# A two-layer diffusion trunk: TensorE's order in both mixers, changed

## The chip, the cores and the metric

The kernel runs on one core of one Trainium2 chip. TensorE (PE) multiplies matrices, VectorE (DVE), ScalarE (ACT) and GpSimd (POOL) do the rest, and SyncE (SP) issues the transfers. The metric is the device time of one launch in microseconds (us). Three runs of the kernel before took 1543.56, 1544.5 and 1545.21 us; the median is 1544.5.

## The reference

The reference is one step of a trunk with two layers, for 128 context tokens and 256 latent tokens, 1024 wide. Each layer is half a SwiGLU, two mixers side by side whose outputs share one projection, and half a SwiGLU again; each sublayer is modulated by a condition.

```
layer 0: h += swiglu(...)/2;  h += [GQA with qk-RMSNorm and axial rotary || bidirectional mLSTM] @ W_mix;   h += swiglu(...)/2
layer 1: h += swiglu(...)/2;  h += [2-D neighbourhood attention with bias || sliding-window GQA with sink] @ W_mix;  h += swiglu(...)/2
attention:  s = q @ k.T * scale (+ bias, + sink column);  p = softmax(s);  o = p @ v
```

Every attention has 8 heads of 64. Latent queries read latent keys (a window of them in layer 1) and 128 cached context keys; context queries read the context alone. The mLSTM replaces the softmax by a decay: exp of differences of cumulated gate logs, forward and backward, times q @ k.T.

## The kernel before

**Tiles and weights.** Tokens lie in three tiles of 128: T=0 is the context, T=1 and T=2 are latent. Weights are streamed: a transfer on SP brings a block into one of three `raw` buffers, ACT makes its high part `whi` (line 121) and DVE or POOL the low part `wlo` (line 122), and each product is three matmuls of 384 columns (lines 378 to 380): high times high, low times high, high times low. One such triple is a *step*; 8 triples, 24 matmuls, make one projection of 128 features (`feat_major`, tile `fm`).

**What sets the order.** A scheduler orders the instructions of each engine by a simulated timeline. Inside a region `in_order` (line 61) the instructions of the engines named are chained in the order in which the code issues them; here that is TensorE. The first mixer has no such region, the loop of the second has one.

**First mixer (layer 0, 300 to 505 us).** The table `ORDER0` (line 30) lists its parts: `k` projects the query tile of two mLSTM heads (`qk_b`, line 934; the copy to `qb` at line 935 and the stacked halves `ksb`, `qdb`), `p` is mLSTM part 1, with `decay` for each head (line 959: two tiles D from `sel` and a mask, then six exponentials on ACT, line 973), `g` the output gate, `f` part 2, `a` the attention of a pair of heads, `m` the output projection. The same table sets the order of the weight blocks. Ahead of it the queries and keys of the attention are normalised, rotated by `rope` (line 610, three operations on DVE for each call) and *turned*: transposed by TensorE into tile `tr` and split into high and low halves `qs`, `ks` on ACT and DVE (lines 645 to 690).

**Second mixer (layer 1, 1069 to 1245 us).** There are 24 attention items: four pairs of heads of sliding-window attention, then four of neighbourhood attention, each with T=1, T=2 and T=0 in this order. An item has three parts (`attn`, line 695): *scores* (tile S, and behind it on DVE and ACT the bias or the sink, the maximum `nm`, the exponential, the sum, and the scaling of E at line 633), *turn* (E transposed into `pt`, line 719, and copied to PT by ACT), and *output* (PT times values into a part of the first `pt` bank, line 732, then split by ACT and DVE into `ych`, `ycl` or `ydh`, `ydl`, lines 636 to 638). Two banks hold `pt`. Between the parts, `fill(n)` sets n steps of other projections (first `fm`, later `mo`). `FILL` gives their numbers for T=1, T=2 and T=0.

Of the kernel before, what the change touches and what calls it, by code (L numbers as in the profile page):

```python
# [6 lines left out]
F32 = mybir.dt.float32  # L7
# [19 lines left out]

ORDER0 = "k0 p0 k1 p1 a0 g0 f0 a1 k2 p2 g1 f1 a2 k3 p3 g2 f2 a3 g3 f3 m0"  # L30

FILL = ((1, 2), (1, 2), (0, 1))
BIG = 1e30


# [101 lines left out]
def body(ctx, tc, d):  # L137
# [469 lines left out]
    def heads(ap, n=64):  # L607
        return ap.rearrange("p (h e) -> p h e", e=n)

    def rope(pool, src, ct, st, nh, nw=4):  # L610

        u, v = work(pool, 512, bufs=nw), work(pool, 512, bufs=nw)
        n = nh * 64
        nc.vector.tensor_tensor(heads(u[:, :n]), heads(src), ct[:, None, :].to_broadcast([P, nh, 64]), op=ALU.mult)
        s4 = src.rearrange("p (h a e) -> p h a e", a=2, e=32)[:, :, ::-1, :]
        v4 = v[:, :n].rearrange("p (h a e) -> p h a e", a=2, e=32)
        t4 = st.rearrange("p (a e) -> p a e", a=2)[:, None, :, :].to_broadcast([P, nh, 2, 32])
        nc.vector.tensor_tensor(v4, s4, t4, op=ALU.mult)
        nc.vector.tensor_tensor(u[:, :n], u[:, :n], v[:, :n], op=ALU.add)
        return u[:, :n]  # L620

    def soft(pool, S, n, nk):

# [139 lines left out]
    def run(steps):  # L763
        finish()
        for _ in steps:
            pass
# [9 lines left out]
    def mixer0():  # L776
        with ExitStack() as es:
# [12 lines left out]
            vctx = m0v[:, 309:437]  # L790
            cbd = m0v[:, 437:1477].rearrange("p (a b) -> p a b", a=4)


            o = token_major(h, 288)
            kv = mp.tile([P, 3, 256], F32, name="kv")
# [97 lines left out]
            for T in TS:  # L893
                for w, (src, nh, h0) in enumerate(((qr[:, T], 8, 0), (kv[:, T, 0:128], 2, 8))):
                    rs = ss[:, T, h0:h0 + nh, None].to_broadcast([P, nh, 64])
                    nc.vector.tensor_tensor(heads(src), heads(src), rs, op=ALU.mult)
                    if T == 0:
                        nc.vector.tensor_tensor(heads(src), heads(src), qkg[:, w, None, :].to_broadcast([P, nh, 64]),
                                                op=ALU.mult)
                        if w == 1:  # L900
                            nc.sync.dma_start(d["k0"], src)
                        r = src
                    else:
                        r = rope(mp, src, cg[:, T - 1, w], sg[:, T - 1, w], nh)
                    (sk.queries if w == 0 else sk.keys)(r, T)

            YA = [(mp.tile([P, NT], F32R, name=f"yah{i}"), mp.tile([P, NT], F32R, name=f"yal{i}")) for i in range(4)]
            YB = []
# [10 lines left out]

            va = mp.tile([P, 3, 8, 65], F32, name="va")  # L920
            nc.vector.memset(va[:, :, :, 64:65], 1.0)
            o = token_major(h, 512)
            for T in range(3):
                nc.scalar.activation(va[:, T, :, 0:64], heads(o[T]), AF.Copy)
            qb = mp.tile([P, 4, NT], F32, tag="qb", name="qb")
            og = mp.tile([P, 4, NT], F32, tag="qo", name="og")

# [5 lines left out]

            def qk_b(i):
                nc.scalar.activation(qb[:, i], feat_major(h), AF.Copy)
                ks = mp.tile([P, 2, NT], F32R, tag="ksb", name="ksb", bufs=1)
                qd = mp.tile([P, 2, NT], F32R, tag="qdb", name="qdb", bufs=1)
                for j in range(2):
                    stack_q(ks[:, j], kb[:, i], j, 1.0)
                    stack_k(qd[:, j], qlb[0][:, j], qb[:, i], j, lambda d, s: nc.gpsimd.tensor_copy(d, s))  # L940
                qkb[i] = ks, qd, qlb[0]

            wst = mp.tile([P, 8, 2], F32, name="wst")
            hst = {}
            sel = mp.tile([P, 64], F32R, name="sel")
            nc.vector.tensor_tensor(sel, ident[:, 0:64], ident[:, 64:128], op=ALU.add)
            mmb = mp.tile([P, 2, 3 * P], BF, name="mmb")
            nc.vector.tensor_copy(mmb.rearrange("p d (b t) -> p d b t", b=3), mmask[:, :, None].to_broadcast([P, 2, 3, P]))
            headg2 = mp.tile([P, 4], F32, name="headg2")
            nc.vector.tensor_scalar(headg2, headg, 0.5, None, op0=ALU.mult)  # L950


            MASKED = ((0, 0, 1), (0, 2, 4), (1, 0, 3))
# [5 lines left out]
            def decay(hd):  # L959
# [14 lines left out]
                nc.vector.tensor_copy(wst[:, hd], E.rearrange("p a n -> p (a n)")[:, 127:513:385])  # L974
                return E

            def part1(i):
                H = work(mp, 780, "H", 780, 2).rearrange("p (t x e) -> p t x e", t=3, e=65)
                for j in range(2):
                    hd = 2 * i + j  # L980
                    b = slice(64 * j, 64 * j + 64)
                    Hj = H[:, 1:3, 2 * j:2 * j + 2]
                    E = decay(hd)
                    pin = bank("ml", "pin")
                    for T in (1, 2):
                        nc.tensor.matmul(pin[:, (T - 1) * 130:T * 130], qb[b, i, T * P:(T + 1) * P],
                                         cbd[b, i, 130 * j:130 * j + 130], start=True, stop=True)
                    ks, qd, ql = [t[:, j] for t in qkb[i]]
                    products(pin[:, 260:388], ks[:, 0:P], qd[:, 0:P], ql[:, 0:P], P)
                    nc.vector.tensor_tensor(Hj, pin[:, 0:260].rearrange("p (t x e) -> p t x e", t=2, e=65),  # L990
                                            wi[:, :, hd, :, None].to_broadcast([P, 2, 2, 65]), op=ALU.mult)
                    nc.vector.tensor_tensor(E[:, :, 0:P], E[:, :, 0:P], pin[:, None, 260:388].to_broadcast([P, 2, P]),
                                            op=ALU.mult)
                    S = bank("ml", "Sm")
                    for o, T in ((0, 2), (256, 1)):
                        products(S[:, o:o + 256], ks[:, T * P:(T + 1) * P], qd[:, P:NT], ql[:, P:NT], 256)
                    nc.vector.tensor_tensor(E[:, 0, P:512], E[:, 0, P:512], S[:, 0:384], op=ALU.mult)
                    nc.vector.tensor_tensor(E[:, 1, P:512], E[:, 1, P:512], S[:, P:512], op=ALU.mult)
                    pv = bank("ml", "pv")
                    for dr, T, terms in TERMS:  # L1000
                        x = ((T - 1) % 3 * 2 + dr) * 65
                        for n, (blk, vt) in enumerate(terms):
                            nc.tensor.matmul(pv[:, x:x + 65], E[:, dr, blk * P:(blk + 1) * P], va[:, vt, hd, :],
                                             start=n == 0, stop=n == len(terms) - 1)
                    nc.vector.tensor_tensor(Hj, Hj, pv[:, 0:260].rearrange("p (t x e) -> p t x e", t=2, e=65), op=ALU.add)
                    nc.scalar.activation(H[:, 0, 2 * j:2 * j + 2], pv[:, 260:390].rearrange("p (x e) -> p x e", e=65), AF.Copy)
                den = H[:, :, :, 64]
                rec = mp.tile([P, 3, 4], F32, tag="rec", name="rec", bufs=2)
                nc.vector.scalar_tensor_tensor(rec, den, -1.0, den, op0=ALU.mult, op1=ALU.max)
                nc.vector.tensor_tensor(rec, rec, emx[:, :, 2 * i:2 * i + 2, :].rearrange("p t h d -> p t (h d)"), op=ALU.max)  # L1010
                nc.vector.reciprocal(rec, rec)
                nc.vector.tensor_tensor(H[:, :, :, 0:64], H[:, :, :, 0:64], rec[:, :, :, None].to_broadcast([P, 3, 4, 64]),
                                        op=ALU.mult)
                H5 = H.rearrange("p t (h d) e -> p (t h) d e", d=2)
                hs = H5[:, :, 0, 0:64]
                nc.vector.tensor_tensor(hs, hs, H5[:, :, 1, 0:64], op=ALU.add)
                hst[i] = hs
# [16 lines left out]
                nc.scalar.activation(og[:, i], feat_major(h), AF.Tanh, scale=0.5)  # L1034
                nc.vector.tensor_scalar(og[:, i], og[:, i], 1.0, None, op0=ALU.add)

            steps = {"a": attn_a, "k": qk_b, "p": part1, "g": out_gate, "f": part2, "m": lambda i: run(mix_out(0, YA, False))}
            for st in ORDER0.split():
                steps[st[0]](int(st[1]))
            for i in range(4):  # L1040
                if i == 0:
# [22 lines left out]
    def mixer1():  # L1064
        with ExitStack() as es:
# [82 lines left out]
            items = [it for i in range(4) for it in swa(i)] + [it for i in range(4) for it in na(i)]  # L1148
            ws.every = 1
            with in_order(tc, (nc.tensor.engine,)):  # L1150
                for it in items[:2]:
                    fill(2)
                    it[0]()
                fill(2)
                for n, (_, turned, output) in enumerate(items):
                    if n in (6, 8):
                        na_keys(n // 2 - 3)
                    turned()
                    fill(FILL[n % 3][0])
                    if n + 2 < len(items):  # L1160
                        items[n + 2][0]()
                        if n + 2 > 12 and (n + 2) % 3 == 2 and n < 18:
                            na_keys((n + 2) // 3 - 2)
                    output()
                    fill(FILL[n % 3][1])
                for _ in weights:
                    pass
            ws.every = EVERY
# [188 lines left out]
```

## Time and profile before

| | |
|---|---|
| median of three runs | 1544.5 us |
| the profiled execution | 1544.31 us |
| its span | 1542.5 us |
| TensorE busy | 1506.3 us, 98% |
| DVE, ACT, POOL busy | 1139.0, 687.7, 146.2 us |
| mean granted clock of TensorE | 0.992 |

How to read the rows below. A timeline row has the start, the duration, the engine, the line, the operation, out<-in with shapes, the number of instructions joined in the row, and in brackets the idle time before it with what ended it. Matmuls overlap: a new one can start while the one before it drains, so durations of neighbours add to more than the distance of their starts. A row of grouped waits has the engine, the tile and line that waited, what it waited for, the sum in us, the count, and the longest. [...] A row of grouped instructions ends with the count, the busy time, the mean ns of one, and the idle time before them.

### The profile page before, as it was taken

The numbers are of one execution on the slowest core, as the hardware profiler recorded it, in microseconds if no ns is written. First come the engines' busy times: TensorE is split into PE (matmuls) and PEld (weight loads), VectorE is DVE, ScalarE is ACT, GpSimd is POOL, SyncE is SP. The second block draws the span as 40 slices with busy tenths as digits, with TensorE's granted clock in tenths as the row PEclk, the third lists the DMA queues.
The fourth block names the chain that finished last, engine by engine and source line by source line (L and its number), as shares of the span: only waits on it lengthen the run. The fifth ranks groups of instructions, "written<-read, shape, count | busy, mean of one in ns | idle before, by whom it ended". The sixth has DMA issues, their size and how long they took to land.

```text
span 1542.5 us, 23066 instructions
## 1 busy us (share of the span) xinstructions
PE 1506.3 (98%) x8888; PEld 1452.2 (94%) x8888; DVE 1139.0 (74%) x2174; ACT 687.7 (45%) x1334; POOL 146.2 (9%) x130
## 2 busy tenths in 40 slices
PE   7999999999999999999999999999998999999997
PEld 5999999997888999999999999999887799999997
DVE  3799999977787899999459899954857777444333
ACT  4543333365664643333345433333667555333321
POOL 2100000124021200000000000001222220000010
PEclk9999999999899999999999999999999999999999
DMA  9645766543012546665354666634431223333331
GB/s 368 237 182 209 264 238 253 200 137 132 28 40 76 214 156 240 250 242 218 114 211 168 216 235 259 242 115 156 140 120 42 69 102 118 137 109 137 120 126 42
DMA packets 40655, 256.91 MB, mean 167 GB/s; under 512 B 4448, under 2 KB 8544, under 8 KB 11232
## 3 DMA queue, kind: packets, MB, share of 16 engines
q1 hardware_dynamic: 40544, 255.43, 45.7%
q8 instruction: 70, 1.15, 0.3%
q14 instruction: 41, 0.34, 0.1%
HBM read 252.52 MB, written 2.89 MB: 166 GB/s over the span
## 4 chain that ended last, share of the span: by engine, by line
PE 94%; DVE 3%; issue 1%; ACT 1%; DMA 0%; POOL 0%; POOLq 0%; SPq 0%; DVEq 0%; ACTq 0%
PE gu L378 16%; PE gu L379 16%; PE gu L380 16%; PE fo L378 8%; PE fo L379 8%; PE fo L380 8%; PE pt L732 2%; PE tm L589 2%; PE tm L590 2%; PE tm L591 2%; PE mo L378 2%; PE mo L379 1%; PE mo L380 1%; PE pt L719 1%; PE fm L378 1%
## 5 line engine op out<-in xcount | busy, mean ns | idle before, releaser
L121 ACT ACTIVATE whi<-raw 128x1024 fp32r<-128x1024 f32 (+2 forms) x378 | 344.3, 927 | 629.7 <-issue 203.8
L122 DVE TENSOR_TENSOR wlo<-raw,whi 128x1024 fp32r<-128x1024 f32 (+2 forms) x335 | 372.0, 1118 | 192.3 <-ACT whi L121 191.3
L378 PE MATMUL gu<-mh,whi 128*128 128x384 f32 x976 | 328.5, 337 | 1.4 <-ACT whi L121 1.4
L379 PE MATMUL gu<-ml,whi 128*128 128x384 f32 x976 | 328.3, 336 | 0.0
L380 PE MATMUL gu<-mh,wlo 128*128 128x384 f32 x976 | 327.5, 336 | 0.0
L256 DVE SCALAR_TENSOR_TENSOR junk<-adaw,cond 128x1024 bf16<-128x1024 f32 x256 | 312.7, 1221 | 2.1 <-DMA adaw<-ada 0.4
L379 PE MATMUL fo<-gl,whi 128*128 128x384 f32 x704 | 235.1, 334 | 0.0
L380 PE MATMUL fo<-gh,wlo 128*128 128x384 f32 x704 | 235.1, 334 | 0.0
L378 PE MATMUL fo<-gh,whi 128*128 128x384 f32 x704 | 235.1, 334 | 0.0
L378 PEld LDWEIGHTS gu<-mh,whi 128*128 128x128 f32 x976 | 183.2, 188 | 2.3 <-ACT whi L121 2.3
L379 PEld LDWEIGHTS gu<-ml,whi 128*128 128x128 f32 x976 | 183.2, 188 | 0.0
L380 PEld LDWEIGHTS gu<-mh,wlo 128*128 128x128 f32 x976 | 183.2, 188 | 0.0
L378 PE MATMUL gu<-hh,whi 128*128 128x386 f32 x432 | 150.0, 347 | 1.4 <-ACT hh L350 1.4
L292 POOL TENSOR_TENSOR ssq<-ssq,sq 128x384 f32<-128x384 f32 x43 | 49.1, 1141 | 1055.3 <-issue 798.9
L379 PE MATMUL gu<-hl,whi 128*128 128x386 f32 x432 | 147.6, 342 | 1.5 <-DVE hl L351 1.5
L380 PE MATMUL gu<-hh,wlo 128*128 128x386 f32 x432 | 146.5, 341 | 0.0
L378 PEld LDWEIGHTS fo<-gh,whi 128*128 128x128 f32 x704 | 132.2, 188 | 0.0
L379 PEld LDWEIGHTS fo<-gl,whi 128*128 128x128 f32 x704 | 132.2, 188 | 0.0
L380 PEld LDWEIGHTS fo<-gh,wlo 128*128 128x128 f32 x704 | 132.2, 188 | 0.0
L378 PEld LDWEIGHTS gu<-hh,whi 128*128 128x128 f32 x432 | 82.2, 190 | 4.9 <-issue 2.9
L379 PEld LDWEIGHTS gu<-hl,whi 128*128 128x128 f32 x432 | 82.2, 190 | 2.0 <-DVE hl L351 2.0
L380 PEld LDWEIGHTS gu<-hh,wlo 128*128 128x128 f32 x432 | 82.2, 190 | 0.0
(294 smaller groups left out, 2098.4 us busy)
## 6 DMA issues: line engine op xcount, KB each, us to landing
adaw<-ada SPq DMA_DIRECT2D x64, 1024.0 KB, 5.5
raw<-f2i SPq DMA_DIRECT2D x44, 1024.0 KB, 4.8
raw<-f1i SPq DMA_DIRECT2D x43, 1024.0 KB, 4.8
raw<-f1o SPq DMA_DIRECT2D x22, 1024.0 KB, 4.7
raw<-f2o SPq DMA_DIRECT2D x22, 1024.0 KB, 4.7
raw<-mo SPq DMA_DIRECT2D x8, 1024.0 KB, 4.8
aw<-aw SPq DMA_DIRECT2D x7, 1024.0 KB, 7.5
raw<-mic SPq DMA_DIRECT2D x6, 1024.0 KB, 4.8
```

The source lines that it names most:

```text
L121: i1 = nc.scalar.activation(hi[:, a:e], src[:, a:e], AF.Copy)
L122: i2 = (self.nc.gpsimd if j % self.every == 0 else self.sub).tensor_tensor(lo[:, a:e], src[:, a:e], hi[:, a:e].bitcast(F32), op=ALU.subtract)
L256: iv = nc.vector.scalar_tensor_tensor(junk, t, 1.0, ada_state["cond"][:, g], op0=ALU.mult, op1=ALU.mult, accum_out=MOD[l][:, j, g, c:c + 1])
L292: nc.gpsimd.tensor_tensor(ssq_t["t"], ssq_t["t"], sq, op=ALU.add)
L378: nc.tensor.matmul(out, wh, xh, start=first, stop=False)
L379: nc.tensor.matmul(out, wh, xl, start=False, stop=False)
L380: return nc.tensor.matmul(out, wl, xh, start=False, stop=last)
L589: nc.tensor.matmul(out[T], hh, wh, start=k == 0, stop=False)
L590: nc.tensor.matmul(out[T], hh, wl, start=False, stop=False)
L591: nc.tensor.matmul(out[T], hl, wh, start=False, stop=k == DC - 1)
L719: nc.tensor.transpose(pt[j * (nb > 1)][:, o:o + P], st["E"][:, j, k * P:(k + 1) * P], ident)
L732: nc.tensor.matmul(y[64 * j:64 * j + 64, :], vals[k](j), PT[:, j, k * P:(k + 1) * P], start=k == 0, stop=k == nb - 1)
```

## The change

In the first mixer a new table `EARLY0` goes ahead of `ORDER0`, and its parts run with TensorE in the order of the code: values, projection k0, the D tiles of head 0, k1, head 1, k2, then the turns of T=1, T=0 and T=2. `rope` writes its result over its source, so that the turns can be issued apart from it. The stacked halves are made in part 1, and three constants earlier. In the second mixer each item sets its steps in one place, between turn and output (2, 2 and 3), and the scores of the item after next follow the output. The numbers of steps in all are unchanged.

```diff
-ORDER0 = "k0 p0 k1 p1 a0 g0 f0 a1 k2 p2 g1 f1 a2 k3 p3 g2 f2 a3 g3 f3 m0"
-FILL = ((1, 2), (1, 2), (0, 1))
+EARLY0 = "v0 k0 d0 k1 d1 k2 t1 t0 t2"
+ORDER0 = EARLY0 + " p0 a0 p1 g0 f0 a1 p2 g1 f1 a2 k3 p3 g2 f2 a3 g3 f3 m0"
+FILL = (2, 2, 3)
...
-        nc.vector.tensor_tensor(u[:, :n], u[:, :n], v[:, :n], op=ALU.add)
-        return u[:, :n]
+        out = u[:, :n] if out is None else out
+        nc.vector.tensor_tensor(out, u[:, :n], v[:, :n], op=ALU.add)
+        return out
...
-                        r = src
                     else:
-                        r = rope(mp, src, cg[:, T - 1, w], sg[:, T - 1, w], nh)
-                    (sk.queries if w == 0 else sk.keys)(r, T)
+                        rope(mp, src, cg[:, T - 1, w], sg[:, T - 1, w], nh, out=src)
+
+            def turn_a(T):
+                sk.queries(qr[:, T], T)
+                sk.keys(kv[:, T, 0:128], T)
...
             def qk_b(i):
                 nc.scalar.activation(qb[:, i], feat_major(h), AF.Copy)
+
+            def stacks_b(i):
                 ks = mp.tile([P, 2, NT], F32R, tag="ksb", name="ksb", bufs=1)
...
+            def decay_early(hd):
+                early[hd] = decay(hd)
+
             def part1(i):
+                stacks_b(i)
...
-                    E = decay(hd)
+                    E = early.pop(hd) if hd in early else decay(hd)
...
+            n0 = len(EARLY0.split())
+            with in_order(tc, (nc.tensor.engine,)):
+                for st in ORDER0.split()[:n0]:
+                    steps[st[0]](int(st[1]))
...
-                for it in items[:2]:
-                    fill(2)
-                    it[0]()
                 fill(2)
+                items[0][0]()
+                fill(1)
+                items[1][0]()
+                fill(3)
...
                     turned()
-                    fill(FILL[n % 3][0])
+                    fill(FILL[n % 3])
+                    output()
                     if n + 2 < len(items):
                         items[n + 2][0]()
...
-                    output()
-                    fill(FILL[n % 3][1])
```

TensorE in the first mixer, before, from the last matmul of the projection k1 on (`fm`). `D` is a decay tile with its mask matmuls, `tr` a turn of rotated queries or keys.

```order
L380 MATMUL fm<-hh_3221,wlo_3705 128x384
L966 MATMUL D<-MS,sel 128x512
L968 LDWEIGHTS identb
L968 MATMUL D<-mmb,identb 128x128
L677 MATMUL tr<-kst,qr 128x128 x4
L968 LDWEIGHTS identb
L968 MATMUL D<-mmb,identb 128x256
L684 MATMUL tr<-kst,kv 128x128
L966 MATMUL D<-MS,sel 128x512
```

The same place in the changed kernel, from the second D tile behind k1 on. The first and the last of the 24 matmuls of k2 are shown.

```order
L978 MATMUL D<-MS,sel 128x512
L980 LDWEIGHTS identb
L980 MATMUL D<-mmb,identb 128x384
L380 MATMUL fm<-hh_3158,whi_3704 128x384
...
L382 MATMUL fm<-hh_3221,wlo_3705 128x384
L680 MATMUL tr<-kst,qr 128x128 x4
L687 MATMUL tr<-kst,kv 128x128
L978 MATMUL D<-MS,sel 128x512
```

The projection k2 now stands between the D tiles and the turns.

TensorE in the second mixer, before, in a group of neighbourhood items: the turn of T=0, scores of T=2, the output of T=0, one step, and the turn of T=1.

```order
L719 MATMUL pt<-kst,E 128x128 x2
L658 MATMUL S<-kdn,qn 128x384
L659 MATMUL S<-kln_10683,qn 128x384
L658 MATMUL S<-kdn,qn 128x384
L659 MATMUL S<-kln_10683,qn 128x384
L732 MATMUL pt<-PT,vc 64x128 x2
L378 MATMUL mo_11848<-ydh_10956,whi_11528 128x384
L379 MATMUL mo_11848<-ydl_10957,whi_11528 128x384
L380 MATMUL mo_11848<-ydh_10956,wlo_11529 128x384
L719 MATMUL pt<-kst,E 128x128 x6
```

The same in the changed kernel; of the three steps the first and the last matmul are shown.

```order
L722 MATMUL pt<-kst,E 128x128 x2
L380 MATMUL mo_11780<-ydh_10960,whi_11350 128x384
...
L382 MATMUL mo_11826<-ydh_10956,wlo_11543 128x384
L735 MATMUL pt<-PT,vc 64x128 x2
L661 MATMUL S<-kdn,qn 128x384
L662 MATMUL S<-kln_10683,qn 128x384
L661 MATMUL S<-kdn,qn 128x384
L662 MATMUL S<-kln_10683,qn 128x384
L722 MATMUL pt<-kst,E 128x128 x6
```

The scores of T=2 now stand directly ahead of the turn of T=1.

DVE in the next group, before: bias and maximum of T=1, an output's split, then T=2's bias and T=1's scaling (`E`).

```order
L711 TENSOR_TENSOR S<-S,rpb 128x256 x2
L628 TENSOR_REDUCE nm<-S 128x1 x2
L638 TENSOR_TENSOR ycl_10967<-pt,ych_10966 128x128
L631 RECIPROCAL sm<-sm 128x2
L711 TENSOR_TENSOR S<-S,rpb 128x256
L633 TENSOR_SCALAR E<-E,sm 128x384 x2
L711 TENSOR_TENSOR S<-S,rpb 128x256
L628 TENSOR_REDUCE nm<-S 128x1
```

The same group in the changed kernel.

```order
L714 TENSOR_TENSOR S<-S,rpb 128x256 x2
L631 TENSOR_REDUCE nm<-S 128x1 x2
L386 SCALAR_TENSOR_TENSOR x_78<-mo_11924,mod_90,x_78 128x256
L386 SCALAR_TENSOR_TENSOR x_78<-mo_11924,mod_90,x_78 128x128
L714 TENSOR_TENSOR S<-S,rpb 128x256 x2
L634 RECIPROCAL sm<-sm 128x2
L631 TENSOR_REDUCE nm<-S 128x1 x2
L636 TENSOR_SCALAR E<-E,sm 128x384 x2
```

T=1's scaling now stands behind both biases and both maxima of T=2.

## Rows read from the trace of the kernel before

**Rows 1.** The page's chain of waits: shares of the span by engine.

```profile
PE 94%; DVE 3%; issue 1%; ACT 1%; DMA 0%; POOL 0%; POOLq 0%; SPq 0%; DVEq 0%; ACTq 0%
```

**Rows 2.** TensorE's grouped waits over the whole run, the two of the first mixer.

```profile
PE tr L684 <- DVE qs L648: 2.6, 2, 2.0
PE D L966 <- ACT qb L935: 2.2, 1, 2.2
```

**Rows 3.** Busy time and granted clock by stretch, first mixer.

```profile
384.90:394.30 9.40, 6.93 (x22) 4.61 (x23) 6.27 (x12) 8.39 (x22) 0.00 (x0) 0.50 0.08 35
```

**Rows 4.** Timeline of TensorE, first mixer, from the projection k1 on.

```profile
374.41 0.39 PE L966 MATMUL D<-MS,sel 128*128 128x512 f32 x1
...
375.09 0.52 PE L966 MATMUL D<-MS,sel 128*128 128x512 f32 x1
...
376.45 0.47 PE L378 MATMUL fm<-hh,whi 128*128 128x384 f32 x1
...
380.78 0.39 PE L966 MATMUL D<-MS,sel 128*128 128x512 f32 x1
...
386.27 0.79 PE L966 MATMUL D<-MS,sel 128*128 128x512 f32 x1 [2.18 <-ACT qb L935]
...
394.35 0.52 PE L378 MATMUL fm<-hh,whi 128*128 128x384 f32 x1
394.67 0.52 PE L379 MATMUL fm<-hl,whi 128*128 128x384 f32 x1
```

**Rows 5.** Timeline of ACT, same stretch.

```profile
380.42 1.87 ACT L973 ACTIVATE w<-D,at 128x128 f32<-128x128 f32 x6 [1.03 <-DVE w L619]
...
382.93 1.87 ACT L973 ACTIVATE w<-D,at 128x128 f32<-128x128 f32 x6
384.65 1.18 ACT L121 ACTIVATE whi<-raw 128x512 fp32r<-128x512 f32 x2
385.69 0.52 ACT L935 ACTIVATE qb<-fm 128x384 f32<-128x384 f32 x1
```

**Rows 6.** TensorE's grouped waits from 1100 to 1236, second mixer.

```profile
PE pt L719 <- DVE ycl L638: 3.7, 4, 1.8
PE pt L732 <- ACT PT L725: 2.0, 3, 1.1
PE pt L719 <- DVE E L633: 1.7, 3, 0.7
PE pt L719 <- DVE ydl L638: 0.6, 1, 0.6
```

**Rows 7.** Timeline of TensorE, second mixer, neighbourhood items.

```profile
1184.66 0.34 PE L659 MATMUL S<-kln,qn 128*128 128x384 f32 x1
...
1187.98 0.52 PE L719 MATMUL pt<-kst,E 128*128 128x128 f32 x3 [0.73 <-DVE E L633]
...
1202.75 0.55 PE L719 MATMUL pt<-kst,E 128*128 128x128 f32 x3 [1.82 <-DVE ycl L638]
...
1204.17 1.12 PE L732 MATMUL pt<-PT,vc 128*64 128x128 f32 x8
...
1207.63 0.82 PE L719 MATMUL pt<-kst,E 128*128 128x128 f32 x6
...
1220.08 0.66 PE L732 MATMUL pt<-PT,vc 128*64 128x128 f32 x8
...
1222.03 0.38 PE L719 MATMUL pt<-kst,E 128*128 128x128 f32 x2
```

**Rows 8.** Busy time and granted clock by stretch, second mixer.

```profile
1204.10:1207.40 3.30, 3.30 (x19) 2.90 (x18) 3.24 (x8) 2.23 (x7) 1.57 (x2) 0.50 0.57 216
```

**Rows 9.** DVE's grouped instructions from 1139 to 1236.

```profile
L633 DVE TENSOR_SCALAR E<-E,sm 128x384 f32<-128x384 f32 x32 | 13.5, 463 | 0.3
L628 DVE TENSOR_REDUCE nm<-S 128x1 f32<-128x385 f32 x16 | 8.6, 555 | 0.3
...
L711 DVE TENSOR_TENSOR S<-S,rpb 128x256 f32<-128x256 f32 x16 | 6.3, 427 | 3.7 <-PE S L659 3.7
```

More of the change, by code (lines that the diff above doesn't have):

```diff
@@ L608, in heads, with rope @@
         return ap.rearrange("p (h e) -> p h e", e=n)
-    def rope(pool, src, ct, st, nh, nw=4):
+    def rope(pool, src, ct, st, nh, nw=4, out=None):
         u, v = work(pool, 512, bufs=nw), work(pool, 512, bufs=nw)
@@ L791, in mixer0 @@
             cbd = m0v[:, 437:1477].rearrange("p (a b) -> p a b", a=4)
+            sel = mp.tile([P, 64], F32R, name="sel")
+            nc.vector.tensor_tensor(sel, ident[:, 0:64], ident[:, 64:128], op=ALU.add)
+            mmb = mp.tile([P, 2, 3 * P], BF, name="mmb")
+            nc.vector.tensor_copy(mmb.rearrange("p d (b t) -> p d b t", b=3), mmask[:, :, None].to_broadcast([P, 2, 3, P]))
+            headg2 = mp.tile([P, 4], F32, name="headg2")
+            nc.vector.tensor_scalar(headg2, headg, 0.5, None, op0=ALU.mult)
             o = token_major(h, 288)
@@ L921, in mixer0, with values_b @@
             nc.vector.memset(va[:, :, :, 64:65], 1.0)
-            o = token_major(h, 512)
-            for T in range(3):
-                nc.scalar.activation(va[:, T, :, 0:64], heads(o[T]), AF.Copy)
+            def values_b(_):
+                o = token_major(h, 512)
+                for T in range(3):
+                    nc.scalar.activation(va[:, T, :, 0:64], heads(o[T]), AF.Copy)
             qb = mp.tile([P, 4, NT], F32, tag="qb", name="qb")
@@ L944, in mixer0 @@
             hst = {}
[L945 to L950, printed above, removed]
             MASKED = ((0, 0, 1), (0, 2, 4), (1, 0, 3))
@@ L1035, in out_gate @@
                 nc.vector.tensor_scalar(og[:, i], og[:, i], 1.0, None, op0=ALU.add)
-            steps = {"a": attn_a, "k": qk_b, "p": part1, "g": out_gate, "f": part2, "m": lambda i: run(mix_out(0, YA, False))}
-            for st in ORDER0.split():
+            steps = {"a": attn_a, "k": qk_b, "p": part1, "g": out_gate, "f": part2, "m": lambda i: run(mix_out(0, YA, False)),
+                     "v": values_b, "d": decay_early, "t": turn_a}
+            n0 = len(EARLY0.split())
+            with in_order(tc, (nc.tensor.engine,)):
+                for st in ORDER0.split()[:n0]:
+                    steps[st[0]](int(st[1]))
+            for st in ORDER0.split()[n0:]:
                 steps[st[0]](int(st[1]))
```

1 line of the change is left out of this document (added).

## Prediction, made before the changed kernel ran

> **What bounds the kernel now.** I read the chain of waits first: 94% of the span is TensorE's own work, DVE adds 3%, ACT 1% [rows 1]. The kernel ends sooner only where TensorE waits less or runs less time at its lower clock. The change touches two places, so I read the grouped waits of TensorE there, then the granted clock, then the timelines of the engines that are waited for.
>
> First mixer: TensorE waits 2.6 us for `qs` (DVE, two waits, the longest 2.0) and 2.2 us once for `qb` (ACT) [rows 2]. [...] The timeline shows the order: the 24 matmuls of the projection k1 run from 376.45 to 380.78, one D tile follows, and the next D tile starts only at 386.27 [rows 4]. Between the two TensorE does little but five turns of queries and keys. The dense matmuls from 394.35 on then come every 0.32 us [rows 4]; the 24 of k1 came every 0.18 us (4.33 / 24). ACT was behind: six exponentials, again six, two halves of a weight piece, and only then the copy of k1's projection at 385.69 [rows 5].
>
> Second mixer: between 1100 and 1236 TensorE waits 8.0 us, 3.7 + 0.6 for the split of an output (`ycl`, `ydl`, whose PSUM bank the next turn needs), 2.0 for PT, 1.7 for scaled probabilities E [rows 6]. Here too the clock is at 0.50 for a while, 1204.1 to 1207.4 [rows 8], just behind the longest wait, 1.82 us [rows 7].
>
> Sums are made against the profiled execution, 1544.31 us (span 1542.5 and 1.8 around it), 0.2 below the median 1544.5. I put the result on the median's scale.
>
> **First mixer, term by term.** TensorE's instructions are the same in number; the order changes. (1) One pair of D tiles and five turns leave the place between k0 and k1, where they took 1.36 us (375.09 to 376.45) [rows 4]; k1 can start at 375.1 and end at 379.4. The pair of D tiles then takes 0.68 (374.41 to 375.09 for a pair), so k2 starts at 380.1 and, with k1's 4.33, ends at 384.4. Then come five turns, 1.36 - 0.68 = 0.68, and a D tile, about 0.4: 385.5. (2) The next D tile shares a bank with the projection and so needs the copy of k2. On ACT the changed order reads: six exponentials, two halves, copy of k1, six exponentials, two halves, copy of k2. The first exponentials start at 380.42 in the profile [rows 5]; I leave that, since they wait for DVE's chain. By the rows: 1.87 for six, 1.04 from the first of the two halves to the copy (384.65 to 385.69), 0.52 for a copy; 380.42 + 2 x 3.43 = 387.3. So TensorE waits about 1.8 us there. (3) At that D tile, the sixth, the kernel before stood at 386.27. The changed one is 1.05 later, has k2 done (4.33) and five turns not (0.68): a gain of 4.33 - 0.68 - 1.05 = 2.6 us. (4) What is late next is ACT again, since decay 2 and 3, whose exponentials stood later, now come here, 1.87 us each. What remained to wait before, 0.6 of the `qs` waits [rows 2], is replaced by several waits that no row shows; bounds are 0 and both packets whole, 3.7; the nearest row is the 0.6, and with more ACT work than there I take 1.5, a loss of 0.9. (5) The clock. Before, 13 dense matmuls came at 0.32 instead of 0.18: 1.8 us sure. From 386.27 to 394.35 there are 8.1 us of small work at half speed; at full speed it would lie between 0 (ACT's chain holds it anyway) and 3.2 us shorter (about 7 us are work, of which full speed needs just over half). I take 1.2. With dense matmuls in the former hole I expect no fall of the clock here: -3.0.
>
> Sum of the first mixer: -2.6 + 0.9 - 3.0 = -4.7 us. Ends: the clock falls all the same and the new waits are whole (-2.6 + 3.1 = +0.5), or nothing of it is paid back and the clock gives all (-2.6 - 5.0 = -7.6).
>
> Costed at nothing: rope writing in place of its source (the same three DVE operations), the three small constants made earlier, the key and query stacks moved into part 1 (their ACT copies leave the crowded stretch), the weights of k2 wanted earlier (SP's order of transfers is unchanged). All hide beside k0 and k1 on TensorE; if that cover failed for the halves of k2's weights, k2 would start later by a pair of halves on ACT, 1.0 us.
>
> **Second mixer, term by term.** Now each item runs turn, steps, output, and then the scores of the item after next. (1) The distance from an item's scores to its own turn shrinks. For T=1 there lay an output and two steps, the turn of T=0, scores, an output and a step; now there lie the turn of T=0, three steps, a small output, and the scores of T=2, directly ahead of the turn. (2) DVE runs in its own order, and in the neighbourhood items that order puts the bias and the maximum of T=2 ahead of the scaling of T=1 in three of four groups; they cannot start before T=2's scores. So TensorE ends the scores of T=2 and waits for bias, maximum and scaling. From below: one bias 0.43, two maxima 1.1, one scaling 0.46 [rows 9], less overlap about 1.7 us. From above: the one group of the kernel before with this order went from the last score matmul (1184.66 + 0.34 = 1185.0) to the turn at 1187.98 [rows 7], 3.0 us, then largely covered by other work. For three groups I take 2.9 (the first, which is that same group), 2.2 and 2.2, and 0.7 for the fourth, where only a bias stands ahead: 8.0 us. (3) The sliding-window items have no bias: a maximum 0.55 and a scaling 0.46 [rows 9], with a short copy of the sink ahead of them, 1.1 us for each of four groups at the most, 0 at the least (the distance may just do). In their order, too, a maximum of T=2 stands ahead of T=1's scaling; I take 1.0 each: 4.0. (4) Of the old 8.0 the waits for PT go, with two or three steps between turn and output; those for an output's bank come from a shorter distance now, one score group instead of one or two steps, but the long waits of (2) lie between and give time; I leave 1.5. (5) There are 24 groups of steps instead of 40, and in place of the 16 changes from an output to steps as many from an output to scores: 0, and no more than the spread below either way. Net: 8.0 + 4.0 + 1.5 - 8.0 = +5.5. (6) The clock. Output and two steps took 3.46 us at 1204.17 to 1207.63 and 1.95 at 1220.08 to 1222.03 [rows 7]: a stretch at the lower clock costs 1.5. It followed one wait of 1.82; with three waits of 2 and more I count two such stretches, one more than before: +1.5. Bounds: none (-1.5), four (+4.5).
>
> [...]
>
> Sum of the second mixer: +7.0. Lower end: 1.7 three times, 0.7, none in (3), 1.5 left, together 7.3 against the old 8.0, so -0.7, and -2.2 if the clock never falls. Upper end: 3.0 three times, 0.7, 4.4 and 1.5, less 8.0, so +7.6, and +12.1 with four stretches.
>
> **Forecast.** -4.7 + 7.0 = +2.3: 1544.5 + 2.3 = 1546.8. Its own range, with one us and a half either way on each mixer, is 1543.8 to 1549.8.
>
> **Rivals.**
> A, slower: the waits for E take the clock down in all four neighbourhood groups. Place: the turns of T=1 there; it decides from the point where the wait right behind the scores of T=2 is over the 1.82 us that did it before. Price: 5.5 + 4.5 = 10 in the second mixer (three stretches more than before), and 2.7 gained in the first (its new waits break the dense work too, so that of the 3.0 of clock 1.0 comes): +7.3, 1551.8. For it: the single fall on record came behind a wait no longer than these. Against: a wait of 1.1 for PT [rows 6] and one of 0.73 [rows 7] brought none.
> B, faster: the second mixer's new order only trades waits, as at its lower bounds (-0.7), and the first gives its 4.7: -5.4, 1539. For it: bias and maximum of the first of the two heads can run beside the second head's scores. Against: the 3.0 us from scores to turn [rows 7].
> C, no change: the sliding-window items do not wait (1.0 in all instead of 4.0, their distance just does), so the second mixer costs 4.0, and the first gives 4.0 to 4.7: 1544.5. For it: all waits for E together were 1.7 us before [rows 6]. Against: the maxima ahead of the scaling.
> That the change does not do what it says has no chance of weight: k2's matmuls stand in the former hole in the changed order.
>
> **Chances and range.** Forecast 0.40, A 0.25, B 0.17, C 0.18. A measurement of this kernel tells 0.2% (3.1 us) from no change. Faster is B and a little of C's lower side, 0.20. Slower is A and a third of the forecast's spread, 0.39. No change takes the rest, 0.41. The range leaves out the far half of B and of A: 1539.5 to 1552.5.
>
> **What would show it.** In the first mixer: no stretch at 0.50 between 380 and 400, 24 dense matmuls of k2 at about 380 to 384.5, then a wait of about 1.8 for the copy `qb`. In the second: waits for PT gone, waits for E of 2 to 3 us at the turns of T=1 in three neighbourhood groups, right behind the scores of T=2, and about 1 us in the sliding-window groups. The forecast is wrong if those waits are under 1 us (then B or C), or if the first mixer still shows a long stretch at 0.50 (then A).

## The result and the profile after

The changed kernel takes 1553.76 us (median of four runs, 1551.66 to 1554.51), the kernel before 1544.72 beside it (four runs). The ratio is 1.0059, 95% interval 1.0046 to 1.0072: slower by 9.0 us. The profiled execution took 1554.51 us with a span of 1552.7. Executions of one kernel differ by up to 5 us; in the version "DVE's order" below the shortest took 1544.45 us at a mean granted clock of TensorE of 0.996, the longest 1549.2 at 0.992.

Three matmuls place the difference: the first of the feed-forward half behind the first mixer, the first step of the second mixer's loop, and the first matmul behind that loop. Timeline of TensorE, the kernel before (start, duration, engine, line, operation):

```profile
508.85 0.33 PE L378 MATMUL gu<-hh,whi 128*128 128x386 f32 x1
...
1138.08 0.34 PE L378 MATMUL fm<-hh,whi 128*128 128x384 f32 x1
...
1248.25 0.33 PE L378 MATMUL gu<-hh,whi 128*128 128x386 f32 x1
```

The same, the changed kernel:

```profile
506.61 0.34 PE L380 MATMUL gu<-hh,whi 128*128 128x386 f32 x1
...
1135.74 0.34 PE L380 MATMUL fm<-hh,whi 128*128 128x384 f32 x1
...
1258.46 0.34 PE L380 MATMUL gu<-hh,whi 128*128 128x386 f32 x1
```

At the end of the first mixer the changed kernel is 2.2 us ahead (508.85 - 506.61). It loses 12.5 in the second mixer's loop: 1258.46 - 1135.74 = 122.7 against 1248.25 - 1138.08 = 110.2. Forecast were -4.7 and +7.0. Between the two and behind the loop the traces differ by 0.1 us at most.

Grouped waits of TensorE in the second mixer, 1080 to 1300, the changed kernel; these answer to [rows 6]:

```profile
PE pt L722 <- DVE E L636: 13.9, 8, 3.9
PE pt L722 <- DVE ydl L641: 1.3, 1, 1.3
PE pt L735 <- ACT PT L726: 0.8, 3, 0.3
```

Together 16.0 us, against 8.0. The waits for `ycl` are gone and those for PT down to 0.8; scaled probabilities E are waited for eight times. Behind the last item, but within the loop's time as counted here, the kernel before also had two waits of together 0.6 us for `x`, which the changed one has not. The turns that wait, and the last score matmul ahead of two of them, in TensorE's timeline; these answer to [rows 7]:

```profile
1187.30 0.34 PE L662 MATMUL S<-kln,qn 128*128 128x384 f32 x1
1191.49 1.51 PE L722 MATMUL pt<-kst,E 128*128 128x128 f32 x6 [3.85 <-DVE E L636]
...
1204.70 0.33 PE L662 MATMUL S<-kln,qn 128*128 128x384 f32 x1
1207.15 1.23 PE L722 MATMUL pt<-kst,E 128*128 128x128 f32 x6 [2.12 <-DVE E L636]
...
1221.95 1.05 PE L722 MATMUL pt<-kst,E 128*128 128x128 f32 x6 [2.27 <-DVE E L636]
...
1232.82 1.05 PE L722 MATMUL pt<-kst,E 128*128 128x128 f32 x6 [0.59 <-DVE E L636]
...
1238.40 1.51 PE L722 MATMUL pt<-kst,E 128*128 128x128 f32 x6 [2.09 <-DVE E L636]
```

Four of the five are the turns of T=1 in the four neighbourhood groups, right behind the scores of T=2. The fifth, at 1238.40, is the turn of T=2 of the last pair. Three turns of T=1 in the sliding-window groups waited 0.94, 0.99 and 1.01 us (13.9 less 3.85, 2.12, 2.27, 0.59 and 2.09 leaves 2.98 for them).

Granted clock of TensorE behind four of these waits (stretch, length, busy time of PE, PEld, DVE, ACT, POOL, then the clock as a share of full speed, the share of DMA, and GB/s); these answer to [rows 8]:

```profile
1191.50:1196.50 5.00, 5.00 (x25) 4.23 (x26) 1.74 (x6) 1.03 (x3) 0.00 (x0) 0.50 0.06 23
1207.30:1210.40 3.10, 3.10 (x14) 2.64 (x15) 0.88 (x4) 0.98 (x2) 0.00 (x0) 0.53 0.86 267
1221.95:1225.40 3.45, 3.44 (x29) 2.81 (x30) 1.33 (x6) 1.24 (x3) 0.00 (x0) 1.00 0.00 0
1238.40:1241.40 3.00, 3.00 (x12) 2.90 (x12) 0.94 (x5) 0.98 (x2) 0.00 (x0) 0.50 0.74 254
```

Summed over the loop, TensorE ran 3.4 us at a granted clock of 0.50 before and 13.7 us now: 6.8 from 1190.4 on, within the wait of 3.85, and 3.4 each behind those of 2.12 and 2.09. Behind the wait of 2.27, longer than two of these, the clock stayed at 1.00.

First mixer: grouped waits of TensorE from 300 to 520, the changed kernel; these answer to [rows 2]:

```profile
PE Sm L661 <- DVE w L1010: 1.9, 2, 0.9
PE D L978 <- ACT qb L951: 1.5, 1, 1.5
PE D L978 <- ACT og L1052: 1.1, 1, 1.1
PE tr L687 <- DVE qs L651: 0.7, 1, 0.7
```

And its clock there; these answer to [rows 3]:

```profile
391.60:395.00 3.40, 3.40 (x11) 3.40 (x12) 0.86 (x2) 1.44 (x5) 0.00 (x0) 0.51 0.00 0
402.00:405.20 3.20, 3.01 (x11) 3.04 (x12) 3.11 (x7) 1.05 (x3) 0.00 (x0) 0.50 0.02 5
```

The long stretch of 385 to 398 is gone, but two short ones, of 3.4 us each, stand in and behind its place.

### The profile page after: what moved, and what is told of

The parts are those of the page before. It is cut to its first block, busy times and chain, and to the rows that moved or that the text cites. A ratio compares the mean times of both kernels' runs of the same rounds, so it can differ in the third digit from the quotient of the medians.

```text
span 1552.7 us, 23075 instructions
## 1 busy us (share of the span) xinstructions
PE 1508.1 (97%) x8888; PEld 1452.7 (94%) x8888; DVE 1140.7 (73%) x2174; ACT 687.7 (44%) x1334; POOL 145.6 (9%) x130
## 4 chain that ended last, share of the span: by engine, by line
PE 93%; DVE 3%; ACT 2%; issue 1%; DMA 0%; POOL 0%; POOLq 0%; SPq 0%; DVEq 0%; ACTq 0%
PE gu L380 16%; PE gu L381 16%; PE gu L382 16%; PE fo L381 8%; PE fo L380 8%; PE fo L382 8%; PE pt L735 2%; PE tm L591 2%; PE tm L592 2%; PE tm L593 2%; PE mo L380 1%; PE pt L722 1%; PE mo L381 1%; PE mo L382 1%; PE S L661 1%
```

## The experiments

All are compared with runs of the kernel before on the same chip. "Loop" is the time from the second mixer's first step to the first matmul behind it, in the trace, 110.2 before and 122.7 in the changed kernel. "Lower clock" is the time at a granted clock of 0.50 within the loop, 3.4 before and 13.7 in the changed kernel; by [rows 7] 3.4 us of it cost 1.5. Where the expectations say 1.2 GHz, this share is meant: the traces show the share, and with it matmuls of 384 columns every 0.32 us [rows 4], 1.2 columns a ns. The runs stood on several chips, on which the kernel before took 1543.38 to 1544.72 us, so versions are set against each other by their ratios; a thousandth is 1.5 us.

**The first mixer's part alone.** The changed kernel with the old loop of the second mixer and the old `FILL`.

```diff
-FILL = (2, 2, 3)
+FILL = ((1, 2), (1, 2), (0, 1))
```

> The kernel before with the first mixer's part of the change alone. Theory: the two parts add up, and the first mixer's trace of the changed kernel (2.3 us less at its end) is this part's whole effect: 1542.4 us, 0.998 to 0.999 of before. Rival (the first mixer's gain hangs on the second, or the transfers that it moves cost later): 1544.5 or more.

Measured: 1541.85 us, ratio 0.9985, interval 0.9976 to 0.9994; a gain of 2.3 us by the ratio, of 1.5 by the medians. In its trace the waits of the first mixer are those of the changed kernel. The first mixer's part is a small gain by itself.

**The second mixer's part alone.** The kernel before with the new loop and the new `FILL`.

> The kernel before with the second mixer's part of the change alone. Theory: 8.0 us more of waits and about 4.5 us more at the lower clock: 1556 to 1557.5 us. Rival (the loss needs both parts, by what reaches the second mixer late or by where the clock's stretches fall): under 1551.

Measured: 1553.3 us, ratio 1.0065, interval 1.0052 to 1.0079: 9.9 slower. Loop 120.0, lower clock 6.8. Its waits for E are again 13.9 us in eight. So the loss is the loop's. The theory's range started 2.7 us higher, and the loop is 2.7 shorter than in the changed kernel: its waits are nearly the same, 15.8 us, but half as much of it is at the lower clock. Stretches in this loop:

```profile
1192.60:1195.90 3.30, 2.94 (x12) 2.96 (x12) 1.37 (x5) 0.98 (x2) 0.00 (x0) 0.50 0.21 82
1196.10:1236.80 40.70, 32.89 (x242) 26.05 (x241) 29.23 (x83) 24.87 (x75) 11.50 (x10) 1.00 0.13 40
```

The second stretch holds waits of 2.13 and 2.27 us at the same turns as in the changed kernel, and the clock fell behind neither. So the same order with the same waits can have 6.8 or 13.7 us at the lower clock.

**DVE's order.** The changed kernel, with every first DVE instruction of an item (bias, sink, maximum) chained behind the scaling of the item before.

```diff
+    def behind(ins):
+        if scaled.get("on") and "old" in scaled:
+            queue_behind(tc, ins, scaled["old"])
...
-            nc.vector.tensor_scalar(E[:, j, :nk], E[:, j, :nk], sm[:, j:j + 1], None, op0=ALU.mult)
+            scaled["new"] = nc.vector.tensor_scalar(E[:, j, :nk], E[:, j, :nk], sm[:, j:j + 1], None, op0=ALU.mult)
...
-                    nc.vector.tensor_tensor(S[j][:, 0:2 * P], S[j][:, 0:2 * P], bias(T)[:, j], op=ALU.add)
+                    behind(nc.vector.tensor_tensor(S[j][:, 0:2 * P], S[j][:, 0:2 * P], bias(T)[:, j], op=ALU.add))
```

> The changed kernel, with DVE told to scale an item's probabilities E before it begins the next item's bias, sink or maximum, in the second mixer's loop alone. Theory (DVE's order, T=2's bias and maxima ahead of T=1's scaling, makes the new waits): the waits for E fall from 13.9 us to under 6, the stretches at the lower clock there to at most one, and the time by 7 to 12 us, to 1542 to 1547. Rival (the distance from scores to turn itself is too short, whatever DVE's order): the waits move to other turns, time within 3 us of 1553.8.

Measured: 1547.42 us, ratio 1.0027, interval 1.0018 to 1.0037: 4.9 us below the changed kernel by the ratios. Loop 115.4, lower clock 3.4. Its waits in the second mixer:

```profile
PE pt L729 <- DVE E L642: 9.2, 10, 1.8
PE pt L729 <- DVE ycl L647: 1.9, 2, 1.7
PE pt L729 <- DVE ydl L647: 1.3, 1, 1.3
```

Its clock in the one stretch of the loop at 0.50:

```profile
1231.00:1234.00 3.00, 3.00 (x14) 2.56 (x15) 0.93 (x5) 1.57 (x6) 0.00 (x0) 0.50 0.94 309
```

Neither came whole: the gain is under the 7 to 12 us of the theory, and E was to be waited for under 6 us. In time, DVE's order makes about half of the loss. The waits lose 3.2 us (16.0 to 12.8, with 0.4 for PT) and their longest falls from 3.85 to 1.77. The lower clock goes from 13.7 to 3.4 in this trace; since it was 6.8 in the part alone with the old waits, how much of that the order brings is not shown. The one fall left came behind a wait of 1.57; behind that of 1.77 there was none. And 9.2 us of waits for E remain, in ten: the distance from scores to turn is too short even where DVE scales ahead of the next item's work.

**Matmuls in the waits.** The changed kernel with nine matmuls ahead of the turn of T=1 in three neighbourhood groups. Their result is overwritten by the turn.

```diff
+            if bias is not None and T == 1 and i < 3:
+                for _ in range(9):
+                    nc.tensor.matmul(pt[1][:, 0:NT], warm["h"][:, 0:P], warm["h"][:, 0:NT], start=True, stop=True)
```

> The changed kernel with nine matmuls of 384 columns, whose result is overwritten, ahead of the turn of T=1 in the first three neighbourhood groups, where TensorE waited 3.9, 2.1 and 2.3 us; nine take about 1.6. Theory (of the loss some 4.5 us are the clock, which falls behind these waits): the waits shrink by what the matmuls take, two or three of the stretches at 1.2 GHz vanish, and the time falls by 2.5 to 4.5 us, to 1549.5 to 1551. Rival (the clock adds nothing that the waits do not cover): within 1 us of 1553.8, or later by what does not fit.

Measured: 1551.56 us, ratio 1.0052, interval 1.0038 to 1.0066: 1.1 us below the changed kernel by the ratios, short of the theory's range; the intervals overlap. Loop 120.3, lower clock 6.8. TensorE's timeline shows the nine matmuls and the turn behind them, in the first two groups:

```profile
1188.27 1.75 PE L723 MATMUL pt<-hh 128*128 128x384 f32 x9
1192.31 1.51 PE L727 MATMUL pt<-kst,E 128*128 128x128 f32 x6 [2.30 <-DVE E L636]
...
1204.59 1.73 PE L723 MATMUL pt<-hh 128*128 128x384 f32 x9
1206.87 0.85 PE L727 MATMUL pt<-kst,E 128*128 128x128 f32 x6 [0.56 <-DVE E L636]
```

Their time comes out of the waits (3.85 to 2.30, 2.12 to 0.56). The clock behind the first falls for a shorter stretch than in the changed kernel, and behind the second not at all:

```profile
1192.50:1195.40 2.90, 2.90 (x12) 2.74 (x11) 0.82 (x3) 0.98 (x2) 0.00 (x0) 0.50 0.06 24
1195.60:1236.00 40.40, 35.72 (x260) 29.17 (x259) 28.80 (x84) 24.84 (x76) 11.07 (x10) 1.00 0.13 40
```

The loop is 2.4 us shorter than in the changed kernel, with 6.9 us of lower clock less. But the second mixer's part alone has no added matmuls and the same picture: loop 120.0, lower clock 6.8, no fall behind its second wait. So that the matmuls kept the clock up is not shown; what is shown is that about 5 us of them (1.75 and twice 1.73) lengthen the loop by no more than 0.2 us against that trace.

**One half of the loop's change: steps in one place, scores ahead of the output.**

```diff
                     fill(FILL[n % 3])
-                    output()
                     if n + 2 < len(items):
                         items[n + 2][0]()
...
+                    output()
```

> The changed kernel, but with the scores of the item after next ahead of the output again; the steps stay in one place (2, 2, 3). It has one half of the loop's change. Theory (scores directly ahead of the turn make the loss): now a small output of 0.5 us lies between T=2's scores and T=1's turn, and DVE begins 0.5 to 1 us earlier for all; the waits for E fall from 13.9 to about 8. But an output now stands directly ahead of a turn that needs its bank: about 0.7 us at each turn of T=1 and T=2, some 10 us of new waits for ycl and ydl. In sum 1552 to 1558. Rival (the steps in one place do no harm of their own): within 3 us of the kernel before plus the first mixer's gain, 1542 to 1545.

Measured: 1553.14 us, ratio 1.0056, interval 1.0042 to 1.007. Loop 122.6, lower clock 10.2. Its waits:

```profile
PE pt L722 <- DVE E L636: 8.0, 6, 2.5
PE pt L722 <- DVE ydl L641: 7.1, 7, 2.0
PE pt L722 <- DVE ycl L641: 5.8, 5, 1.7
```

As the theory had it: the waits for E shrink to 8.0 and those for the bank of an output, which must be split before the next turn, grow to 12.9.

**The other half: steps in two places, scores behind the output.**

```diff
-FILL = (2, 2, 3)
+FILL = ((1, 2), (1, 2), (0, 1))
...
-                    fill(FILL[n % 3])
+                    fill(FILL[n % 3][0])
                     output()
...
+                    fill(FILL[n % 3][1])
```

> The changed kernel, with the steps in the two places of the kernel before (1 and 2, 1 and 2, 0 and 1), and the scores behind the output. It has the other half of the loop's change. Theory: one step lies between T=2's scores and T=1's turn, 0.53 us, two between the others; the waits for E fall to about 9, but the waits for PT come back (2 us and more, since no step lies between T=0's turn and its output). In sum 1549 to 1553. Rival (the place of the scores is harmless once the steps are split): under 1545.

Measured: 1550.05 us, ratio 1.0035, interval 1.0023 to 1.0047. Loop 117.3, lower clock 0. Its waits:

```profile
PE pt L735 <- ACT PT L728: 8.6, 7, 1.8
PE pt L735 <- ACT PT L726: 2.4, 4, 1.0
PE pt L722 <- DVE E L636: 2.0, 3, 0.9
```

The time came inside the theory's range, the split did not: E, put at 9, is hardly waited for; PT is, 11.0 us. Each half costs, by a different wait: the old loop kept a step or scores between a turn and its output, and steps between an output and the next turn. These two runs also allow an estimate of what I had set at nothing, from one trace each and with the price of [rows 7]. With the steps in one place the loop grew by 12.4 while its waits grew by 12.9 (8.0 to 20.9), those for `x` went (0.6), and the lower clock grew by 6.8 (3.0): some 3 us are saved, perhaps by the fewer groups of steps, which is not shown. With the scores behind the output it grew by 7.1, while waits grew by 5.8 (8.0 to 13.8, with 0.8 for `ydl`) and 3.4 of lower clock (1.5) went: some 2.8 us are lost. In the changed kernel the two nearly cancel.

**GpSimd beside DVE.** The changed kernel with the low parts of the weights in the loop made by DVE.

```diff
-            ws.every = 1
+            ws.every = 1 << 30
```

> The changed kernel, with the low parts of the weights in the second mixer's loop made by DVE instead of GpSimd. In the changed kernel's trace DVE instructions that run beside such a GpSimd instruction end when it ends (a 128x2 subtraction took 1.10 us, two scalings 1.80). Theory (GpSimd holds DVE up, and that lengthens two of the long waits for E): these two shrink by 0.9 to 1.4 us each, but DVE gets 16 halves of 0.68 us, 11 us, between its other work; the time stays within 3 us of 1553.8, or rises. Rival (DVE's stretched instructions have nothing to do with GpSimd): they stay as long as they were.

Measured: 1557.0 us, ratio 1.0081, interval 1.0067 to 1.0095. Loop 125.3, lower clock 17.1. In the changed kernel, timeline of DVE and of GpSimd:

```profile
1187.35 1.10 DVE L353 TENSOR_TENSOR hl<-mod,hh 128x2 fp32r<-128x2 f32 x1
...
1190.92 0.75 DVE L636 TENSOR_SCALAR E<-E,sm 128x384 f32<-128x384 f32 x2
...
1236.79 1.80 DVE L636 TENSOR_SCALAR E<-E,sm 128x384 f32<-128x384 f32 x2
```

```profile
1185.92 2.52 POOL L124 TENSOR_TENSOR wlo<-raw,whi 128x512 fp32r<-128x512 f32 x2 [11.95 <-ACT whi L123]
...
1235.55 2.49 POOL L124 TENSOR_TENSOR wlo<-raw,whi 128x512 fp32r<-128x512 f32 x2 [13.97 <-ACT whi L123]
```

With those subtractions on DVE, its timeline has the last scaling and the subtraction `hl` so:

```profile
1189.20 0.16 DVE L353 TENSOR_TENSOR hl<-mod,hh 128x2 fp32r<-128x2 f32 x1
...
1240.94 0.74 DVE L636 TENSOR_SCALAR E<-E,sm 128x384 f32<-128x384 f32 x2
```

The stretched instructions are short again (1.10 to 0.16, 1.80 to 0.74), and the longest wait fell from 3.85 to 3.44, the last from 2.09 to 1.64, each by about half of the least that the theory had. That GpSimd stretched them is shown as far as its absence removes it. DVE's added work costs more than it gives: all waits for E rise from 13.9 to 15.3 us, and the time is 3.4 us over the changed kernel by the ratios.

**k2 left in its old place.** The first mixer's part alone, with k2 out of the early order.

```diff
-EARLY0 = "v0 k0 d0 k1 d1 k2 t1 t0 t2"
-ORDER0 = EARLY0 + " p0 a0 p1 g0 f0 a1 p2 g1 f1 a2 k3 p3 g2 f2 a3 g3 f3 m0"
+EARLY0 = "v0 k0 d0 k1 d1 t1 t0 t2"
+ORDER0 = EARLY0 + " p0 a0 p1 g0 f0 a1 k2 p2 g1 f1 a2 k3 p3 g2 f2 a3 g3 f3 m0"
```

> The first mixer's part of the change alone, but with the projection k2 back behind a1; the early order is values, k0, decay 0, k1, decay 1, and the turns. Theory (k2 fills the hole behind k1, and that is the gain): the hole comes back, some 4 us of waits behind k1, the lower clock lasts 10 us and more again, and the time is that of the kernel before or above, 1.000 to 1.003 of it. Rival (the gain comes from the fixed order and the turns in place): it stays at 0.998 to 0.999.

Measured: 1542.32 us, ratio 0.9992, interval 0.9983 to 1.0001. The two waits of the hole are back, and the lower clock with them:

```profile
PE D L978 <- ACT qb L951: 2.5, 1, 2.5
PE tr L680 <- ACT ks L689: 1.7, 1, 1.7
```

```profile
385.20:395.00 9.80, 7.99 (x24) 6.44 (x25) 3.26 (x7) 6.67 (x21) 0.00 (x0) 0.50 0.09 36
```

The hole is there as the theory said; the time lies between its two answers, 0.7 thousandths above the part with k2, less than the intervals tell apart. Counted from the first matmul of the mixer (tile `pk`, at 304.84 with k2 and 305.55 without) to its end, the traces have 201.4 us with k2 and 202.9 without. The waits are 7.5 and 7.8 in all, so k2 moved waits rather than took them away; the 1.5 us go with 3.4 us less at the lower clock.

**The first output gate early too.** The first mixer's part alone, with g0 between the turns of T=1 and T=0.

```diff
-EARLY0 = "v0 k0 d0 k1 d1 k2 t1 t0 t2"
+EARLY0 = "v0 k0 d0 k1 d1 k2 t1 g0 t0 t2"
```

> The first mixer's part of the change alone, with the projection of the first output gate also moved ahead, between the turns of T=1 and T=0. Theory (the rest of the stretch at 1.2 GHz follows the small waits behind k2; dense work there removes them): the waits of 1.5, 0.7 and 0.4 us for qb, qs and w shrink under 1 in all, one of the two stretches at 1.2 GHz goes, and the time is 1 to 4 us below that of the part alone, 0.996 to 0.998 of before. Rival (ACT is the bound there, and the same waits come later): 0.998 to 0.999, as without.

Measured: 1539.2 us, ratio 0.9965, interval 0.9952 to 0.9979: 5.4 us below the kernel before by the ratio, and the fastest version here; its interval overlaps that of the part alone. The first mixer ends at 504.36. Its waits and its clock in the first mixer:

```profile
PE D L978 <- ACT w L985: 2.2, 3, 1.2
PE Sm L661 <- DVE sm L634: 0.9, 1, 0.9
```

```profile
380.00:400.00 20.00, 16.69 (x95) 13.34 (x94) 13.33 (x24) 17.48 (x46) 3.41 (x3) 1.00 0.30 105
406.00:409.00 3.00, 3.00 (x15) 2.49 (x13) 1.62 (x6) 2.90 (x9) 1.01 (x2) 0.50 0.00 0
```

The waits for `qb` and for the turns' `qs` are gone, as expected; waits for the exponentials (`w`) took 2.2 of their place, so they are not under 1 in all. All waits of the mixer are 5.8 us, against 7.5 in the part alone. The granted clock is 1.00 through the whole place where it had fallen before, and one stretch is left, behind it. That is not g0's doing for certain: in the part alone, too, it fell only from 400.4 and from 407.3 on. Nine traces here have the first mixer of the changed kernel: seven of them have 6.8 us at the lower clock and take 201.3 to 201.6 us from `pk` to the end; two (scores ahead of the output, and the other steps of the last section) have 3.4, with the clock at 1.00 up to 398, and take 199.8. With g0 early it is 198.5 at 3.4. So of the 2.9 against the part alone, 1.3 are left for g0 at an equal clock; they go with the 1.7 us less of waits.

**Two edits of the old loop**, both on the first mixer's part. One takes steps 1 and 2, 1 and 1, 1 and 1; one has the old steps and DVE's order as above.

```diff
-FILL = ((1, 2), (1, 2), (0, 1))
+FILL = ((1, 2), (1, 1), (1, 1))
```

> The first mixer's part of the change with the loop of the kernel before, but steps 1 and 2, 1 and 1, 1 and 1 instead of 1 and 2, 1 and 2, 0 and 1. Theory (the two long waits for PT come from T=0, whose output follows its turn with no step between): these 1.8 us go, the step is missing nowhere, and the time is about 1.5 us below that of the part alone. Rival (with a step less ahead of it T=0's turn waits for the bank of T=2's output): the waits move there, no change.

> The first mixer's part of the change with the loop of the kernel before, and DVE told to scale each item's E before the next item's bias, sink or maximum. Theory (DVE's order makes the waits only where scores stand directly ahead of a turn): E was scaled in time for most items before, 1.7 us of waits; these go, the waits for an output's bank stay or grow, and the time is within 1.5 us of the part alone. Rival (the order is the better one everywhere): 2 us or more below it.

Measured: 1542.43 us, ratio 0.9989 (0.998 to 0.9998), and 1544.12 us, ratio 1.0003 (0.9994 to 1.0012). Neither gains on the part alone, 0.9985. With the other steps, PT is waited for 1.1 instead of 1.8 us and E 3.2 instead of 1.7; the waits moved, though not to the bank as the rival had it. With DVE's order, the waits for an output's bank grow from 4.3 to 6.1, and those for E, which were to go, from 1.7 to 2.2. The loop is 114.0 in its trace against 109.9 in the part alone, at 3.4 us of lower clock in both; by the ratios the order costs 2.8 us, more than the 1.5 of the theory, with intervals that just touch. In the old loop the scheduler's order was the better one.

## Why the prediction was wrong

Slower was likelier than faster, but no change was given the largest chance; the forecast was 1546.8, and the time lies above the range. The loss came as waits for E and as lower clock behind them, which is the mechanism of the forecast and of rival A. A's price, 1551.8, lies nearer, and its three stretches more are what this trace has; but its condition did not hold as stated: of the turns of T=1 in the four neighbourhood groups two took the clock down, one with 2.27 us did not though it is over 1.82, and one fall came at a turn of T=2 that A does not name. That its count fits is luck. Three steps of the sum failed: the waits of the second mixer lacked a turn, its clock was counted too low, and the first mixer's later waits were put too low.

- **Second mixer, waits (2) and (3).** Right in kind and nearly in size: the turns of T=1 behind the scores of T=2, DVE's order, 1 us in the sliding-window groups. Forecast for the four neighbourhood groups were 2.9, 2.2, 2.2 and 0.7, together 8.0; measured 3.85, 2.12, 2.27 and 0.59, together 8.8. The first was longer because two DVE instructions stood ahead of the bias, one that waited 0.82 us for ACT and one stretched to 1.10 beside GpSimd. For the sliding-window groups 4.0 was forecast; 0.94, 0.99 and 1.01 came, 2.9, and one group did not wait. Term (4), 1.5 for an output's bank, measured 1.28 for `ydl`; 0.8 for PT was left, which the sum had at nothing.
- **A term that was missing.** The turn of T=2 of the last pair waited 2.09. Its exponential stood on ACT behind two halves of a weight piece, until 1235.89, and its scaling is the one stretched to 1.80. Net of the old 8.0 the waits grew by 8.0, not 5.5.
- **Second mixer, the clock (6).** This is the largest miss. I counted one stretch at 0.50 more, 3.4 us, for a price of 1.5; there were 10.3 us more. The loop grew by 12.5, of which 8.0 are these waits less 0.6 for `x`; of the remaining 5.1, 10.3 us cost 4.5 by [rows 7], or 3.7 by the same loop with half the lower clock (106.7 and 104.2 us without the waits, a difference of 2.5 for 6.9). What failed is counting falls by the length of a wait: 2.27 us brought none, and the second mixer's part alone, with the same waits, had just the one stretch more that I counted. Why the clock falls behind one wait and not behind an equal one stays open.
- **Term (5), nothing for the changes between kinds of work.** Near in sum, 0.6 to 1.4 us, but by the estimate above as two terms of about 3 us with opposite signs.
- **First mixer, waits (3) and (4).** Up to the sixth D tile the sum held: it started at 387.06 with 1.49 of waiting, forecast 387.3 with 1.8. Then it failed: I let the later waits grow by 0.9; but waits stood even behind the next projection, 1.1 for `og` and 1.9 for `Sm`, where decay tiles, gate and part 1 now meet on ACT and DVE. All waits from 300 to 520 were 6.9 us before (2.6, 2.2, 0.6, 0.6, 0.5, 0.4) and 7.5 after (1.9, 1.5, 1.1, 0.7, 0.6, 0.5 and three of 0.4): no gain of 1.7, a loss of 0.6.
- **First mixer, the clock (5).** Forecast -3.0, and what is left of the 2.2 us gained, when the waits cost 0.6, is -2.8, with 6.8 us less at the lower clock. But it did not come as I put it: the clock still fell, in two shorter stretches, behind the small waits. That the number fits is in part luck: with the same waits two other traces have 3.4 us less of it, and this mixer is 1.6 shorter there.
- **Order of size.** -4.7 was -2.2, and +7.0 was +12.5; both errors have one sign, and both come in part from waits behind the first that I saw.

## What to carry to other kernels

In a loop that alternates small attention work with dense steps, look for what stands directly ahead of each waiting instruction, on both engines: scores directly ahead of a turn, with the next item's maximum ahead of this item's scaling on DVE, cost 8 us of waits here. A wait of TensorE can have a second price behind it, work at a granted clock of 0.50: here about 1.2 to 1.6 us for each stretch of 3.4. But one trace does not tell which wait brings it: before a change of the clock is put down to an edit, look whether another trace with the same order and the same waits has it too. Price a moved wait to the end of its stretch, not to the first place where it is covered.

## What the runs showed of the hardware that was not expected

**Equal waits, unequal clock.** In the feed-forward half behind the first mixer all thirteen traces have the same three waits for a weight piece, 0.34, about 0.7 and 0.33 us within 3 us. In three traces the clock fell behind them, in ten it did not. TensorE right behind these waits, in the first mixer's part alone and then in the kernel before (stretch, length, busy times, clock, as above):

```profile
581.40:584.60 3.20, 3.20 (x11) 3.20 (x11) 3.20 (x5) 0.00 (x0) 0.00 (x0) 0.50 0.81 307
583.90:587.10 3.20, 3.20 (x20) 3.20 (x19) 3.20 (x5) 0.06 (x1) 0.00 (x0) 1.00 0.84 310
```

From the end of the first mixer to the second mixer's loop the three take 630.7 to 630.8 us and the ten 629.1 to 629.2: one stretch of 3.4 us at 0.50 cost 1.6 us in this dense work.

**DVE beside GpSimd.** Three DVE instructions of the changed kernel's loop were stretched while GpSimd made a low part. `hl`, 128x2, took 1.10 us at 1187.35 to 1188.45, with GpSimd busy from 1185.92 to 1188.44; without GpSimd's work it took 0.16. Two scalings of E took 0.75 and 1.47 us instead of 0.42 and ended 0.2 us behind GpSimd's instruction. Others beside it kept their time: the biases (0.43), the maxima (0.55), the splits (0.28) and a reciprocal (0.17 at 1236.59). What sets the three apart from these no run here shows.
